# Low parts of the expert weights: two slabs per expert halved between GpSimd and VectorE, in place of one slab left whole to GpSimd

## Chip, cores and metric

The kernel runs on one core of a Trainium2 chip. The metric is the device time of one execution in microseconds (us), median over several runs. Engines are named PE (TensorE), DVE (VectorE), ACT (ScalarE), POOL (GpSimd) and SP (SyncE, which issues most of the DMAs).

## What is computed

Two transformer-like blocks run one after the other over 1024 tokens of width 1024. The change lies at the end of the second block, in its mixture of experts: 32 experts, two per token, each a gated MLP from 1024 to 512 and back. Cut to what matters:

```
def expert_block(args):
    xb, e = args
    hb = jax.nn.silu(xb @ w_g[e]) * (xb @ w_u[e])
    return hb @ w_d[e]
```

The tokens of an expert are gathered, go through `expert_block`, and come back scaled by their gates. All is float32.

## The kernel before

A float32 product is made from three matmuls of rounded operands (`mm3`, lines 133 to 135): high by high (L133), high by low (L134), low by high (L135). So each operand is split: ACT rounds it to a high part (`ehi`, by `A` on line 40), and the low part is the operand less its high part (`elo`, by `TT` on line 43).

The experts' weights come in **units**, one DMA of 1 MB each: a slab of 128 partitions by 2048 floats. An expert has six, in the order g0, g1 (gate), u0, u1 (up), d0, d1 (down). PE takes them in the order g0, g1, u0, u1 of expert e, then d0, d1 of expert e-1, then g0 of expert e+1, twelve matmuls to a unit. In the middle of g0 stand four transposes of the hidden activations `hb` of the expert before, and behind u0 and behind u1 four each of the gathered tokens `xe` of the next expert.

The order is written out by hand (`tc.manual_schedule()`): at unit i the program first splits unit i+2 (`split_unit`, `AHEAD = HB - 1 = 2`), then issues the matmuls of unit i, then the small work that hangs on it, then the load of the slab whose buffer unit i's place in the ring frees. High and low parts have three buffers each (`HB = 3`); raw slabs lie in a ring of eleven up to unit 150, of six after it. In `esplit` ACT makes `ehi`, and one engine, handed in as `eng`, makes the whole of `elo`: POOL for u1, DVE for the other five units. DVE also makes the low parts `hl` and `xl` of the activations (their first operand lies in PSUM), and the product `hb`. POOL also issues the gather of tokens (L1493) and the scatter of results (L1532), both indirect DMAs, in its own program order. SP issues the slab loads in order (`eload`, L1482); each waits until the readers of the slab that held its buffer are done.

Of the kernel before, what the change touches and what calls it, by code (L numbers as in the profile page):

```python
# [9 lines left out]
F32 = mybir.dt.float32  # L10
# [17 lines left out]
def block_kernel(  # L28
# [8 lines left out]
    pe, act, dve, pool, sp = nc.tensor, nc.scalar, nc.vector, nc.gpsimd, nc.sync  # L37

    def A(o, i, f, **kw):
        act.activation(out=o, in_=i, func=f, **kw)  # L40

    def TT(o, a, b, op, eng=None):
        (eng or dve).tensor_tensor(out=o, in0=a, in1=b, op=op)  # L43

    def TS(o, a, s1, op0, s2=None, op1=None, eng=None):
        if op1 is None:
            (eng or dve).tensor_scalar(out=o, in0=a, scalar1=s1, scalar2=None, op0=op0)
        else:
            (eng or dve).tensor_scalar(out=o, in0=a, scalar1=s1, scalar2=s2, op0=op0, op1=op1)

    def STT(o, a, s, b, op0, op1, **kw):
        dve.scalar_tensor_tensor(out=o, in0=a, scalar=s, in1=b, op0=op0, op1=op1, **kw)  # L52

    MUL, ADD, SUB, MAX, MIN, POW = (
        ALU.mult, ALU.add, ALU.subtract, ALU.max, ALU.min, ALU.pow)
# [10 lines left out]
    def bank(tag, bufs):  # L66
        return ps[0].tile([128, 512], F32, name=tag, tag=tag, bufs=bufs)

    def mmb():
        return bank("mm", 2)  # L70

    def tpb():
        return bank("tp", 2)
# [28 lines left out]
    def split(hi, lo, src, scale=None):  # L102
        if scale is None:
            A(hi, src, AF.Copy)
            TT(lo, src, hi.bitcast(F32), SUB)
        else:
            A(hi, src, AF.Identity, scale=scale)
            STT(lo, src, scale, hi.bitcast(F32), MUL, SUB)
# [22 lines left out]
    def mm3(o, l, r, start, stop):  # L131

        pe.matmul(out=o, lhsT=l[0], rhs=r[0], start=start, stop=False)  # L133
        pe.matmul(out=o, lhsT=l[0], rhs=r[1], start=False, stop=False)  # L134
        pe.matmul(out=o, lhsT=l[1], rhs=r[0], start=False, stop=stop)  # L135

    def fslice(n=HALF):

        t = big.tile([128, 2, HALF], F32R, name="fs", tag="fs", bufs=NB)
        return t[:, 0, 0:n], t[:, 1, 0:n]  # L140
# [272 lines left out]
    with ExitStack() as ad_stack:  # L413
# [3 lines left out]
        for g in range(G):  # L417
            was.append([])
            for i in range(8):
                raw = adp.tile([128, 2, 1024 // G], F32, name="wa", tag="wa", bufs=8 * G)  # L420
# [6 lines left out]
        for k in range(8):  # L427
            o = tpb()
# [6 lines left out]
        for k in range(8):  # L435
            gk = 8 // G
            j = k % gk
            if j == 0:
                acc = adp.tile([128, 2, 1024 // G], F32, name="acc", tag="acc", bufs=2)
                for i in range(8):  # L440
                    w = was[k // gk][i]
# [4 lines left out]
                o = mmb()  # L446
# [6 lines left out]
            hi, lo = fslice()  # L453
# [1008 lines left out]
    def table(pos, rhs, n, out_i):  # L1462

        o = bank("gu", 4)
        for i in range(2):
            m = ew.tile([128, 8, 128], F32R, name="mt_", tag="ys", bufs=2)
            TT(m, islot[:, None].to_broadcast([128, 8, 128]),
               pos[:, 8 * i:8 * i + 8, None].to_broadcast([128, 8, 128]), ALU.is_equal)
            for j in range(8):
                pe.matmul(out=o[:, 0:n], lhsT=m[:, j], rhs=rhs(8 * i + j), start=(i + j == 0), stop=(i + j == 8))  # L1470
        A(out_i, o[:, 0:n], AF.Identity, scale=-1.0, bias=twos)
# [8 lines left out]
    def eload(src, nm="eraw"):  # L1480
        raw = rings[nm][0].tile([128, 2048], F32, name=nm, tag=nm, bufs=rings[nm][1])
        sp.dma_start(out=raw, in_=src)  # L1482
        return raw

    def esplit(raw, eng):
        hi = ew.tile([128, 2048], F32R, name="ehi", tag="ehi", bufs=HB)
        lo = ew.tile([128, 2048], F32R, name="elo", tag="elo", bufs=HB)
        A(hi, raw, AF.Copy)
        TT(lo, raw, hi.bitcast(F32), SUB, eng=eng)
        return hi, lo  # L1490

    def gather(xe, itok):
        pool.indirect_dma_start(out=xe, out_offset=None, in_=xn_d[:, :],  # L1493
                                in_offset=bass.IndirectOffsetOnAxis(ap=itok, axis=0),
                                bounds_check=S - 1, oob_is_err=False)

    def x_tile():
        return [mo2.tile([128, 8, 128], F32R, name=n_, tag=n_, bufs=2) for n_ in ("xh", "xl")]

    def x_part(xe, xs, g):  # L1500
        tp = bank("tpe", 2)
        transpose4(tp, [xe[:, (g * 4 + i) * 128:(g * 4 + i + 1) * 128] for i in range(4)])
        split(xs[0][:, g * 4:g * 4 + 4], xs[1][:, g * 4:g * 4 + 4], tp.rearrange("p (k n) -> p k n", k=4))

    def up_half(o, xs, w, half, mid=None):

        for i in range(4):
            k = 4 * half + i
            mm3(o, (xs[0][:, k], xs[1][:, k]), [p_[:, i * 512:(i + 1) * 512] for p_ in w], k == 0, k == 7)
            if i == 1 and mid is not None:  # L1510
                mid()

    def h_tile():
        return [mo.tile([128, 4, 128], F32R, name=n_, tag=n_, bufs=2) for n_ in ("hh", "hl")]

    def h_part(tp, hb):
        transpose4(tp, [hb[:, i * 128:(i + 1) * 128] for i in range(4)])

    def y_bank():
        return ps[0].tile([128, 2, 512], F32, name="yo", tag="yo", bufs=1)  # L1520

    def down_half(yo, hs, w, half):
        for i in range(2):
            k = 2 * half + i
            for n in range(2):
                c0 = i * 1024 + n * 512
                mm3(yo[:, n], (hs[0][:, k], hs[1][:, k]), [p_[:, c0:c0 + 512] for p_ in w], k == 0, k == 3)

    def scatter(yo, irow):
        ys = ew.tile([128, D], F32, name="ys", tag="ys", bufs=2)  # L1530
        A(ys, yo.rearrange("p a n -> p (a n)"), AF.Copy)
        pool.indirect_dma_start(out=y_d[:, :], out_offset=bass.IndirectOffsetOnAxis(ap=irow, axis=0),  # L1532
                                in_=ys, in_offset=None, bounds_check=2 * S - 1, oob_is_err=False)
# [9 lines left out]
    for i in range(len(units)):  # L1543
        nm = wide[i % len(wide)] if i < WIDE else "eraw"
# [7 lines left out]
    raws = {}  # L1552
# [22 lines left out]
    parts, banks, hbs, hss, tps, xss, yos = {}, {}, {}, {}, {}, {}, {}  # L1575

    def split_unit(i):
        nm, e, half = units[i]
        parts[i] = esplit(raws.pop(i), pool if (nm, half) == ("u", 1) else dve)

    with tc.manual_schedule():
        for e in range(2):
# [5 lines left out]
        for i in range(AHEAD):  # L1588
            split_unit(i)
        for i, (nm, e, half) in enumerate(units):  # L1590
            if i + AHEAD < len(units):
                split_unit(i + AHEAD)
            w = parts.pop(i)
            if nm in "gu":
                if half == 0:
                    banks[nm, e] = bank("gu", 4)
                if (nm, half) == ("g", 0) and e:
                    def mid():
                        tps[e - 1] = bank("tpe", 2)
                        h_part(tps[e - 1], hbs.pop(e - 1))  # L1600
# [51 lines left out]
    with tc.For_i(0, rounds) as r_:  # L1652
        with tc.For_i(0, NE) as e_:
            pos = ew.tile([128, 16], F32, name="pos", tag="pos", bufs=1)
            TS(pos, posk, shift, SUB)
            ti = ew.tile([128, 2], I32, name="ti", tag="ti", bufs=1)
            table(pos, lambda j: tkr[:, j], 2, ti)
            gather(xes[0], ti[:, 0:1])
            xs = x_tile()
            for g in range(2):  # L1660
                x_part(xes[0], xs, g)
            gu = []
            for w in (w_e_gate_2, w_e_up_2):
                o = bank("gu", 4)
                for half in range(2):
                    up_half(o, xs, esplit(eload(w[bass.ds(e_, 1), half].rearrange("o p n -> (o p) n")), dve), half)
                gu.append(o)
            hb = ew.tile([128, 512], F32, name="hb", tag="hb", bufs=2)
            A(hb, gu[0], AF.Silu)
            TT(hb, hb, gu[1], MUL)  # L1670
            tp = bank("tpe", 2)
            h_part(tp, hb)
            hs = h_tile()
            split(*hs, tp.rearrange("p (k n) -> p k n", k=4))
            yo = y_bank()
            for half in range(2):
                down_half(yo, hs, esplit(eload(w_e_down_2[bass.ds(e_, 1), half].rearrange("o p n -> (o p) n")), dve),
                          half)
            scatter(yo, ti[:, 1:2])
            TS(shift, shift, 1024.0, ADD)  # L1680
        TS(shift, shift, float(C - NE * 1024), ADD)
# [51 lines left out]
```

## Time and profile before

| | us |
|---|---|
| median of 3 runs | 2148.75 |
| lowest, highest | 2148.54, 2151.77 |
| the profiled execution, its own time | 2150.52 |
| span of the profiled execution | 2148.8 |
| busy PE | 1961.3 (91% of the span) |
| busy DVE | 1446.0 (67%) |
| busy ACT | 1177.3 (55%) |
| busy POOL | 632.5 (29%) |

The experts fill the span from about 1480 to 2090 us. In all views a time is a start in us from the beginning of the span, followed by a duration; a bracket at a row's end tells how long the engine had been idle just before the instruction, and on which engine's instruction it had waited. A busy PE says little by itself, since matmuls overlap: the distance from one start to the next tells what a matmul costs.

### The profile page before, as it was taken

The numbers are of one execution on the slowest core, as the hardware profiler recorded it, in microseconds if no ns is written. First come the engines' busy times: TensorE is split into PE (matmuls) and PEld (weight loads), VectorE is DVE, ScalarE is ACT, GpSimd is POOL, SyncE is SP. The second block draws the span as 40 slices with busy tenths as digits, with TensorE's granted clock in tenths as the row PEclk, the third lists the DMA queues.
The fourth block names the chain that finished last, engine by engine and source line by source line (L and its number), as shares of the span: only waits on it lengthen the run. The fifth ranks groups of instructions, "written<-read, shape, count | busy, mean of one in ns | idle before, by whom it ended". The sixth has DMA issues, their size and how long they took to land.

```text
span 2148.8 us, 32901 instructions
## 1 busy us (share of the span) xinstructions
PE 1961.3 (91%) x12914; PEld 1653.1 (77%) x12914; DVE 1446.0 (67%) x1923; ACT 1177.3 (55%) x1868; POOL 632.5 (29%) x522
## 2 busy tenths in 40 slices
PE   3999899999999999999999999995999999999980
PEld 2878796887777988889887997894777777777760
DVE  6476774656687754686557855746777777877765
ACT  3454553445465533564335634643777777777752
POOL 3362110144453000241004300003444444344425
PEclk8999999999997999999999999996999999999995
DMA  9212334621111263212622156464999999999956
GB/s 295 70 50 57 111 90 137 193 78 40 31 40 30 60 191 90 64 45 85 191 59 59 51 161 205 157 245 178 347 366 361 379 355 357 358 360 354 360 202 240
DMA packets 218934, 381.60 MB, mean 178 GB/s; under 512 B 50165, under 2 KB 173077, under 8 KB 193177
## 3 DMA queue, kind: packets, MB, share of 16 engines
q1 hardware_dynamic: 194520, 345.79, 46.9%
q10 hardware_dynamic: 15040, 16.89, 2.3%
q0 software_dynamic: 9216, 16.80, 2.1%
q8 instruction: 102, 1.67, 0.3%
q14 instruction: 56, 0.45, 0.1%
HBM read 356.35 MB, written 39.85 MB: 184 GB/s over the span
## 4 chain that ended last, share of the span: by engine, by line
PE 51%; issue 25%; POOL 9%; DVE 7%; DMA 6%; ACT 3%; POOLq 0%; ACTq 0%; SPq 0%; DVEq 0%; another core or an unknown queue 0%
PE mm L133 11%; PE mm L134 11%; PE mm L135 11%; POOL xe L1493 3%; PE tp L189 3%; POOL y_d L1532 2%; PE z L741 1%; DMA xp<-u_d 1%; PE sc L1139 1%; PE sc L1168 1%; PE at L599 1%; PE at L601 1%; PE os L770 1%; DVE wlo L43 1%; DVE kp L43 1%
## 5 line engine op out<-in xcount | busy, mean ns | idle before, releaser
L43 DVE TENSOR_TENSOR elo<-eraw,ehi 128x2048 fp32r<-128x2048 f32 x160 | 402.0, 2528 | 131.2 <-ACT ehi L40 131.2
L40 ACT ACTIVATE ehi<-eraw 128x2048 fp32r<-128x2048 f32 x192 | 366.9, 1912 | 18.8 <-PE yo L135 12.6
L133 PE MATMUL mm<-whi,fs 128*128 128x256 f32 x1152 | 335.4, 293 | 0.9 <-ACT whi L40 0.9
L134 PE MATMUL mm<-wlo,fs 128*128 128x256 f32 x1152 | 334.4, 291 | 0.8 <-DVE wlo L43 0.8
L135 PE MATMUL mm<-whi,fs 128*128 128x256 f32 x1152 | 331.1, 289 | 0.0
L43 DVE TENSOR_TENSOR wlo<-raw,whi 128x1024 fp32r<-128x1024 f32 x156 | 198.6, 1273 | 148.3 <-ACT whi L40 146.7
L40 ACT ACTIVATE whi<-raw 128x1024 fp32r<-128x1024 f32 x156 | 164.8, 1056 | 214.8 <-PE mm L134 93.9
L133 PEld LDWEIGHTS mm<-whi,fs 128*128 128x128 f32 x1152 | 225.0, 196 | 9.0 <-issue 5.5
L134 PEld LDWEIGHTS mm<-wlo,fs 128*128 128x128 f32 x1152 | 225.6, 196 | 8.1 <-issue 6.0
L135 PEld LDWEIGHTS mm<-whi,fs 128*128 128x128 f32 x1152 | 224.2, 195 | 2.4 <-issue 2.3
L134 PE MATMUL gu<-elo,xh 128*128 128x512 f32 x512 | 207.1, 405 | 15.9 <-POOL elo L43 14.4
L133 PE MATMUL gu<-ehi,xh 128*128 128x512 f32 x512 | 208.0, 406 | 2.5 <-ACT ehi L40 2.5
L133 PE MATMUL mm<-fs,whi 128*128 128x512 f32 x480 | 197.2, 414 | 7.5 <-DVE mst L43 4.1
L135 PE MATMUL gu<-ehi,xl 128*128 128x512 f32 x512 | 202.9, 396 | 0.0
L134 PE MATMUL mm<-fs,whi 128*128 128x512 f32 x480 | 197.0, 410 | 1.2 <-DVE fs L52 1.2
L135 PE MATMUL mm<-fs,wlo 128*128 128x512 f32 x480 | 195.1, 406 | 0.0
L43 POOL TENSOR_TENSOR elo<-eraw,ehi 128x2048 fp32r<-128x2048 f32 x32 | 147.6, 4612 | 97.2 <-ACT ehi L40 97.2
L134 PEld LDWEIGHTS gu<-elo,xh 128*128 128x128 f32 x512 | 96.6, 189 | 47.1 <-POOL elo L43 24.6
L133 PEld LDWEIGHTS mm<-fs,whi 128*128 128x128 f32 x480 | 94.0, 196 | 39.4 <-issue 9.6
L133 PEld LDWEIGHTS gu<-ehi,xh 128*128 128x128 f32 x512 | 96.7, 189 | 23.8 <-ACT ehi L40 2.9
L135 PEld LDWEIGHTS gu<-ehi,xl 128*128 128x128 f32 x512 | 96.5, 189 | 21.5
L135 PEld LDWEIGHTS mm<-fs,wlo 128*128 128x128 f32 x480 | 94.2, 196 | 23.4 <-issue 4.0
(467 smaller groups left out, 4234.5 us busy)
## 6 DMA issues: line engine op xcount, KB each, us to landing
eraw<-in_w_e_up_dram SPq DMA_DIRECT2D x64, 1024.0 KB, 7.1
eraw<-in_w_e_down_dram SPq DMA_DIRECT2D x64, 1024.0 KB, 7.3
eraw<-in_w_e_gate_dram SPq DMA_DIRECT2D x64, 1024.0 KB, 7.6
raw<-in_w_in_dram SPq DMA_DIRECT2D x92, 512.0 KB, 3.8
raw<-in_w_out_dram SPq DMA_DIRECT2D x32, 512.0 KB, 3.5
wa<-in_w_ada_dram SPq DMA_DIRECT2D x16, 512.0 KB, 5.9
fy<-y_d SPq DMA_DIRECT2D x8, 1024.0 KB, 8.7
xt<-in_x_dram SPq DMA_DIRECT2D x8, 512.0 KB, 5.6
```

The costliest lines, as they stand in the source:

```text
L40: act.activation(out=o, in_=i, func=f, **kw)
L43: (eng or dve).tensor_tensor(out=o, in0=a, in1=b, op=op)
L133: pe.matmul(out=o, lhsT=l[0], rhs=r[0], start=start, stop=False)
L134: pe.matmul(out=o, lhsT=l[0], rhs=r[1], start=False, stop=False)
L135: pe.matmul(out=o, lhsT=l[1], rhs=r[0], start=False, stop=stop)
L189: pe.transpose(o[0:s.shape[-1], j * 128:j * 128 + s.shape[0]], s, ident[0:s.shape[0], 0:s.shape[0]])
L599: pe.matmul(out=ov[:, hh, ch], lhsT=full[:, hh, ch], rhs=v(ch, hh), start=True, stop=s0 is None)
L601: pe.matmul(out=ov[:, hh, ch], lhsT=qs[r, ch * 128:(ch + 1) * 128], rhs=s0[r], start=False, stop=True)
L741: pe.matmul(out=zp[:, 0:w], lhsT=qc[r, pr, t * 128:(t + 1) * 128], rhs=kc_full[r, pr, s0 * 128:s0 * 128 + w], start=True, stop=True)
L770: pe.matmul(out=os_[:, hd * 64:hd * 64 + 64], lhsT=pt[:, j * 128:(j + 1) * 128], rhs=vc_full[:, s0 + j, hd * 64:hd * 64 + 64], start=(hd = ...
L1493: pool.indirect_dma_start(out=xe, out_offset=None, in_=xn_d[:, :], in_offset=bass.IndirectOffsetOnAxis(ap=itok, axis=0), bounds_check=S - ...
L1532: pool.indirect_dma_start(out=y_d[:, :], out_offset=bass.IndirectOffsetOnAxis(ap=irow, axis=0), in_=ys, in_offset=None, bounds_check=2 * S ...
```

## The change

`esplit` takes a column `n` in place of an engine. POOL makes the low part of the columns from `n` on, DVE that of the columns before `n`. For u1 and for d1, `n` is 1024; for the other units it is 2048, so that DVE makes the whole and POOL nothing. ACT's part is the same.

```diff
-    def esplit(raw, eng):
+    def esplit(raw, n=2048):
+
         hi = ew.tile([128, 2048], F32R, name="ehi", tag="ehi", bufs=HB)
         lo = ew.tile([128, 2048], F32R, name="elo", tag="elo", bufs=HB)
         A(hi, raw, AF.Copy)
-        TT(lo, raw, hi.bitcast(F32), SUB, eng=eng)
+        if n < 2048:
+            TT(lo[:, n:], raw[:, n:], hi[:, n:].bitcast(F32), SUB, eng=pool)
+        TT(lo[:, 0:n], raw[:, 0:n], hi[:, 0:n].bitcast(F32), SUB)
         return hi, lo
...
     def split_unit(i):
         nm, e, half = units[i]
-        parts[i] = esplit(raws.pop(i), pool if (nm, half) == ("u", 1) else dve)
+        parts[i] = esplit(raws.pop(i), 1024 if (nm, half) in (("u", 1), ("d", 1)) else 2048)
```

The loop over further rounds of experts, which this input does not enter, calls `esplit` with its default and is the same as before.

POOL's queue over one expert in the middle of the stage, before (gather and scatter of the expert before, low part of u1, gather, scatter):

```order
L1493 DMA xe_14940<-xn_d,idt 128x1024 [waits DMASW6_49,PE_49]
L1532 DMA y_d<-ys,idt 2048x1024 [waits DMASW1_49,Activation_49]
L43 TENSOR_TENSOR elo<-eraw,ehi 128x2048 [waits DMAHW6_49,Activation_49]
L1493 DMA xe_14939<-xn_d,idt 128x1024 [waits DMASW0_49,PE_49]
L1532 DMA y_d<-ys,idt 2048x1024 [waits DMASW3_49,Activation_49]
```

and with the change (scatter, half of u1, half of d1, gather, scatter):

```order
L1535 DMA y_d<-ys,idt 2048x1024 [waits DMASW1_49,Activation_49]
L43 TENSOR_TENSOR elo<-eraw,ehi 128x1024 [waits DMAHW6_49,Activation_49]
L43 TENSOR_TENSOR elo<-eraw,ehi 128x1024 [waits DMAHW0_49,PE_49,Activation_49]
L1496 DMA xe_14939<-xn_d,idt 128x1024 [waits DMASW0_49,PE_49]
L1535 DMA y_d<-ys,idt 2048x1024 [waits DMASW3_49,Activation_49]
```

The 2048 columns of u1 have become 1024, and 1024 of d1 stand between them and the gather.

DVE's queue with the change, over one expert: low part of u0, `hl`, half of u1, low part of d0, `xl`, half of d1, `hb`, `xl`, low part of the next g0:

```order
L43 TENSOR_TENSOR elo<-eraw,ehi 128x2048 [waits DMAHW3_49,PE_49,Activation_49]
L43 TENSOR_TENSOR hl<-tpe,hh 128x512 [waits Activation_49]
L43 TENSOR_TENSOR elo<-eraw,ehi 128x1024 [waits DMAHW4_49,Activation_49]
L43 TENSOR_TENSOR elo<-eraw,ehi 128x2048 [waits DMAHW5_49,PE_49,Activation_49]
L43 TENSOR_TENSOR xl<-tpe,xh 128x512 [waits Activation_49]
L43 TENSOR_TENSOR elo<-eraw_15759,ehi 128x1024 [waits DMAHW6_49,Activation_49]
L43 TENSOR_TENSOR hb<-hb,gu 128x512 [waits PE_49]
L43 TENSOR_TENSOR xl<-tpe,xh 128x512 [waits Activation_49]
L43 TENSOR_TENSOR elo<-eraw_15780,ehi 128x2048 [waits DMAHW7_49,Activation_49]
```

Before, the row of u1 was not there, and that of d1 had 2048 columns; nothing else moved on DVE.

PE's queue with the change at the beginning of u1. Before, the first matmul that reads `elo` waited for POOL:

```order
L133 MATMUL gu<-ehi,xh 128x512 [waits Activation_49]
L134 MATMUL gu<-elo,xh 128x512 [waits DVE_49]
L135 MATMUL gu<-ehi,xl 128x512
L133 MATMUL gu<-ehi,xh 128x512
L134 MATMUL gu<-elo,xh 128x512
L135 MATMUL gu<-ehi,xl 128x512
L133 MATMUL gu<-ehi,xh 128x512
L134 MATMUL gu<-elo,xh 128x512 [waits Pool_49]
```

Now the first waits for DVE, whose half holds its columns, and the third, six matmuls later, for POOL. The same pair of waits stands at d1. The order of the matmuls is the same as before.

## Rows read from the trace of the kernel before

**Rows 1.** The page's first line: span of the profiled execution.

```profile
span 2148.8 us, 32901 instructions
```

**Rows 2.** Waits of PE, 1480 to 2090: total us, times, longest.

```profile
PE gu L134 <- POOL elo L43: 14.4, 32, 0.9
```

**Rows 3.** Timeline of PE: start, us, engine, line, operation, operands, idle before.

```profile
1705.22 0.39 PE L133 MATMUL gu<-ehi,xh 128*128 128x512 f32 x1
...
1714.41 0.47 PE L133 MATMUL gu<-ehi,xh 128*128 128x512 f32 x1
1715.32 0.50 PE L134 MATMUL gu<-elo,xh 128*128 128x512 f32 x1 [0.43 <-POOL elo L43]
...
1718.34 0.48 PE L133 MATMUL yo<-ehi,hh 128*128 128x512 f32 x1
1718.65 0.39 PE L134 MATMUL yo<-elo,hh 128*128 128x512 f32 x1
...
1724.03 0.39 PE L133 MATMUL gu<-ehi,xh 128*128 128x512 f32 x1
1724.26 0.40 PE L134 MATMUL gu<-elo,xh 128*128 128x512 f32 x1
...
2071.79 0.40 PE L133 MATMUL gu<-ehi,xh 128*128 128x512 f32 x1
2073.07 0.50 PE L134 MATMUL gu<-elo,xh 128*128 128x512 f32 x1 [0.89 <-POOL elo L43]
```

**Rows 4.** Timeline of POOL: first a gather before the stage, then one expert.

```profile
1478.48 0.99 POOL L1493 DMA_INDIRECT xe<-xn_d,idt  x1 [4.21 <-PE tpe L189]
...
1710.66 4.60 POOL L43 TENSOR_TENSOR elo<-eraw,ehi 128x2048 fp32r<-128x2048 f32 x1 [2.77 <-ACT ehi L40]
1718.86 2.26 POOL L1493 DMA_INDIRECT xe<-xn_d,idt  x1 [3.59 <-PE tpe L189]
```

**Rows 5.** Timeline of DVE in the same expert: `hl`, d0, d1, g0.

```profile
1710.49 0.68 DVE L43 TENSOR_TENSOR hl<-tpe,hh 128x512 fp32r<-128x512 f32 x1
1713.90 3.52 DVE L43 TENSOR_TENSOR elo<-eraw,ehi 128x2048 fp32r<-128x2048 f32 x1 [2.72 <-ACT ehi L40]
...
1717.94 2.28 DVE L43 TENSOR_TENSOR elo<-eraw,ehi 128x2048 fp32r<-128x2048 f32 x1
...
1721.34 2.27 DVE L43 TENSOR_TENSOR elo<-eraw,ehi 128x2048 fp32r<-128x2048 f32 x1
```

**Rows 6.** Timeline of ACT in the same expert: high parts of u1, d0, d1, g0.

```profile
1708.66 1.92 ACT L40 ACTIVATE ehi<-eraw 128x2048 fp32r<-128x2048 f32 x1
...
1711.95 1.91 ACT L40 ACTIVATE ehi<-eraw 128x2048 fp32r<-128x2048 f32 x1
...
1715.18 1.91 ACT L40 ACTIVATE ehi<-eraw 128x2048 fp32r<-128x2048 f32 x1
...
1719.11 1.91 ACT L40 ACTIVATE ehi<-eraw 128x2048 fp32r<-128x2048 f32 x1
```

**Rows 7.** Kernel's end: timelines of DVE and POOL; POOL by tile `x3t` (min/median/max ns).

```profile
2112.92 4.57 DVE L52 SCALAR_TENSOR_TENSOR x3t<-fy,pk,x3t 128x1024 f32<-128x1024 f32 x2
2113.40 3.01 POOL L43 TENSOR_TENSOR x3t<-x3t,nfw 128x1024 f32<-128x1024 f32 x1 [1.27 <-ACT x3t L40]
L43 POOL TENSOR_TENSOR x3t<-x3t,nfw x4: 2344/3021/3037, 2113.4 to 2140.5; 128x1024 f32<-128x1024 f32 x4
```

**Rows 8.** By tile `wlo`, earlier stages: DVE subtraction of 1024 columns (min/median/max ns).

```profile
L43 DVE TENSOR_TENSOR wlo<-raw,whi x156: 1187/1224/2287, 15.9 to 1414.7; 128x1024 fp32r<-128x1024 f32 x156
```

**Rows 9.** Windows: busy us of each engine, granted PE clock, DMA share, GB/s.

```profile
1762.00:1780.80 18.80, 18.37 (x86) 14.67 (x85) 14.79 (x10) 14.26 (x12) 8.01 (x3) 1.00 1.00 393
1686.80:1987.60 300.80, 293.82 (x1343) 234.74 (x1343) 236.72 (x145) 228.50 (x176) 128.29 (x48) 1.00 0.94 360
```

**Rows 10.** SP's waits, 1500 to 2080; landing of `eraw`, 1930 to 2060.

```profile
SPq L1482 <- DVE elo L43: 380.8, 145, 6.5
...
DMA to landing us min/median/max: 6.5/7.5/9.4
```

More of the change, by code (lines that the diff above doesn't have):

```diff
@@ L1665, in block_kernel @@
                 for half in range(2):
-                    up_half(o, xs, esplit(eload(w[bass.ds(e_, 1), half].rearrange("o p n -> (o p) n")), dve), half)
+                    up_half(o, xs, esplit(eload(w[bass.ds(e_, 1), half].rearrange("o p n -> (o p) n"))), half)
                 gu.append(o)
@@ L1676, in block_kernel @@
             for half in range(2):
-                down_half(yo, hs, esplit(eload(w_e_down_2[bass.ds(e_, 1), half].rearrange("o p n -> (o p) n")), dve),
-                          half)
+                down_half(yo, hs, esplit(eload(w_e_down_2[bass.ds(e_, 1), half].rearrange("o p n -> (o p) n"))), half)
             scatter(yo, ti[:, 1:2])
```

## Prediction

> **What bounds it now.** The page's span [rows 1] says how long, not why, so I went first to PE's waits inside the experts' stage. They are nearly one line: 32 times, once per expert, PE waits for the low part of u1 that POOL makes [rows 2]. That row counts only idle time; what a wait costs is read from starts. In the timeline of PE the first two matmuls of u1 start 0.91 us apart (1714.41 and 1715.32). The first two of d0, which also follow four transposes but wait for nothing, start 0.31 us apart [rows 3]. So an expert loses 0.91 - 0.31 = **0.60 us**. The last expert has no transposes there: 1.28 us (2071.79 to 2073.07) against the 0.23 us of a plain pair (1724.03 to 1724.26), so it loses 1.05 us [rows 3]. All else on PE is back to back: 18.81 us per expert (1705.22 to 1724.03), at a granted clock of 1.00, the 2.4 GHz level [rows 3, 9].
>
> The timeline of POOL shows why: its 2048 columns take 4.60 us and end at 1715.26, 0.06 us before PE goes on [rows 3, 4]. The timeline of DVE shows a second thing. Its low part of d0 starts at 1713.90, while POOL is still at u1, and takes 3.52 us; the next one, beside no subtraction of POOL, takes 2.28 [rows 5]. From POOL's end to its own end are 2.16 us, so during the overlap it did almost nothing. `hl`, with an operand in PSUM, starts at 1710.49, overlaps POOL as well, and keeps its 0.68 us [rows 4, 5].
>
> **Who blocks whom.** Since the change starts both engines on one slab, this decides. The end of the kernel shows both directions [rows 7]. DVE runs two operations from 2112.92 to 2117.49. POOL starts in the middle of the first, at 2113.40, and needs 3.01 us where the same operation alone takes 2.34: it had to wait 0.67 us, until 2114.07, about the end of DVE's first. DVE's second then ends 1.08 us behind POOL's end at 2116.41. So two operations that read two SBUF operands run one after the other, and the one that was waiting first goes first.
>
> The Trainium skill says the same in "SBUF — State Buffer", section "Who interferes with whom": a VectorE instruction with two SBUF inputs and a GpSimd instruction that reads SBUF exclude each other for the whole instruction, and the first to issue wins. "Perfetto Trace Analysis", section "Optimizing Scalar/DVE Operations", concludes from it that moving work between the two might not help, which speaks against this change; by it the sum below would shrink to that of the first rival.
>
> **The change, u1.** POOL's half takes 2.34 us by the one that ran alone [rows 7]; half of the 4.60 of now would be 2.30 [rows 4]. DVE's half takes 1.19 us alone [rows 8], or 1.08 behind POOL [rows 7]. The bounds for a ready first half are thus 1.19 us (POOL loses) and 2.34 + 1.08 = 3.42 us (POOL wins). At u1 DVE is at `hl` when the high part comes, so I take the upper end: POOL from 1710.66 to 1713.00, DVE done at 1714.08. PE wants it 0.31 us after its start at 1714.41, at 1714.72: **0.6 us to spare, the stall goes**. POOL's half is wanted six matmuls later still. d0 follows on DVE at about 1714.0 and, with POOL silent, ends near 1716.3 in place of 1717.4.
>
> **The change, d1.** This is the added cost. Before, DVE alone made d1 (1717.94 to 1720.22), then `hb` and `xl` in 1.12 us, and from 1721.34 g0 of the next expert, without a gap [rows 5]. Now `xl` is done by about 1716.9, ACT's high part of d1 ends at 1717.09 [rows 6], and both engines stand ready. Who goes first? Behind ACT's high part DVE's d0 started within 0.04 us (1713.86 to 1713.90), POOL's u1 within 0.08 (1710.58 to 1710.66) [rows 4 to 6]. No row shows a tie, so there are two bounds:
> - DVE first: its half ends at 1717.13 + 1.19 = 1718.32. POOL's runs to 1718.32 + 2.34 = 1720.66, beside `hb` and `xl`, which do not collide. The high part of g0, ready 0.60 us earlier than before at 1719.11 - 0.60 + 1.91 = 1720.42 [rows 6], lets DVE start g0 at 1720.66 and end it near 1722.9. PE wants it at 1724.26 - 0.60 = 1723.66: 0.7 us to spare.
> - POOL first: POOL 1717.17 to 1719.51, DVE's half done at 1720.59. Then come `hb` and `xl` (1.12 us), and g0 runs from 1721.71 to 1723.98; with the 0.06 us that PE took behind POOL it goes on at 1724.04, 0.38 us late.
>
> I take DVE first. At this place DVE has nothing left in front of it, and it wakes sooner.
>
> **What else moves.** The gather on POOL now stands behind d1's half: it would start near 1720.7 and not 1718.86 [rows 4]. Its tokens are wanted nearly two experts later, so nobody waits. It may hold DVE off g1 for about the 0.89 us that its end lay behind DVE's before (1720.22 to 1721.12) [rows 4, 5]; g1 is wanted a whole unit after g0, so I cost that at nothing; without this cover it would be up to 0.89 us per expert. SP's load behind d1 is released by POOL, some 0.4 us later than by DVE. Slabs land within 9.4 us [rows 10] and one ring turn of six units is about an expert of 18 us, so the load has several us left. PE's extra wait at the third low matmul is over before PE comes to it. SP spends 380.8 us waiting for buffers [rows 10]: loads are not what is late.
>
> **The sum.** 31 stalls of 0.60 us and one of 1.05 us are 19.6 us. In the first expert `hb` is late on DVE by itself; I leave 0.2 us there. That makes 19.4 us less than the profiled execution's own 2150.52, or 2131.1. The median of the three runs is 1.77 us lower, so the forecast is 2148.75 - 19.4 = **2129.3 us**.
>
> **Rivals.**
> - *POOL wins at d1.* PE's stall moves from u1 to the next g0 and shrinks to 0.38 us. The gain is 31 x 0.22 + 1.05 = 7.9 us: 2140.9. For it: at the kernel's end POOL, once waiting, went ahead of DVE [rows 7]. Against: the quicker start just named. This is where the skill's remark on moving work would come true.
> - *The transfers take the gain.* An expert in 18.21 us and not 18.81 asks for 360 x 18.81 / 18.21 = 372 GB/s. If the queues could give no more than the 360 of now [rows 9], nothing would be won: 2148.8. For it: the DMA share is 0.94. Against: a stretch with share 1.00 moved 393 GB/s [rows 9].
> - *The gather holds the port (slower).* Place: POOL wins d1, the gather follows at once behind DVE's half (1720.59) and keeps DVE out. From 1.34 us on (to 1721.93: g0 is due at 1721.71, and 0.22 us are left of the stall removed) the kernel is slower than before. If it kept the port for all its 2.26 us [rows 4], to 1722.85, g0 would end at 1725.12 and PE go on 0.92 us later than before: 31 x 0.92 - 1.05 = 27.5 us more, 2176.2. Against: an unhindered gather takes 0.99 us in all [rows 4], and the 2.26 holds 1.36 us of waiting for DVE.
> - *The change does nothing for u1*, if PE still waited for both halves at its first low matmul. The order has it wait for DVE's half there and for POOL's at the third, and POOL's would be in time even for the first. I give it no chance of its own.
>
> **Chances.** DVE first at d1, the forecast: 0.72. POOL first: 0.15. Transfers, or a gain given back elsewhere: 0.08. The gather, or another collision: 0.05. A measurement here tells about 0.2% (4.3 us) from no change; POOL first lies 3.6 us beyond that, and I count 0.10 of its 0.15 as faster, since its own spare times are estimates. Faster 0.82, same 0.13, slower 0.05. The range goes from 2127.5 (the stalls' full 19.6 us and a little for other runs) to 2143.0, which takes in POOL first and 2 us beside it, as the unknown order of the two at d1 wants.
>
> **What would show it.** Right: PE's waits lose the line of rows 2; u1's first two matmuls start 0.31 us apart; POOL's instructions in `elo` are 64, those at d1 near 3.5 us from start to end since they wait for DVE's 1.2; an expert takes 18.2 us. Wrong: a new line of PE waiting for DVE's `elo` at g0, with DVE's halves at d1 near 3.4 us (POOL first); ACT waiting for slabs to land (transfers); DVE's g0 or g1 near 3 us or more beside a gather (port).

## The result, and the profile after

| | before | changed |
|---|---|---|
| median, first comparison (4 and 4 runs) | 2148.64 us | 2122.81 us |
| lowest, highest | 2147.08, 2151.77 | 2118.66, 2127.94 |
| median, second comparison (17 and 6 runs) | 2148.27 us | 2126.93 us |
| profiled execution: span, granted clock | 2148.8 us, 0.949 | 2120.9 us, 0.953 |

The ratio is 0.9893, with a 95% interval from 0.9871 to 0.9916, and in the second comparison 0.9898 (0.9876 to 0.9920). The kernel became faster by about 22 us. The forecast was 2129.3 us; the first median lies 6.5 us below it and under the range, the second lies 2.4 us below it, which is also under the range (its lower end was 2127.5).

PE's waits in the experts' stage come first, as they did before (engine, what it waited for, us in total, times, longest):

```profile
PE gu L133 <- ACT ehi L40: 2.5, 1, 2.5
PE gu L134 <- DVE elo L43: 1.5, 1, 1.5
PE yo L135 <- DVE hl L43: 1.5, 1, 1.5
PE yo L133 <- ACT hh L40: 1.2, 1, 1.2
PE tpe L189 <- DVE hb L43: 0.8, 1, 0.8
```

The line of [rows 2], 32 waits for POOL, is gone, and what is left are single waits at the first and the last expert. The timeline of PE shows the same place as [rows 3]: the matmul that opens an expert, the four transposes ahead of u1, u1's first three matmuls, and the opening matmul of the next expert.

```profile
1707.51 0.39 PE L133 MATMUL gu<-ehi,xh 128*128 128x512 f32 x1
...
1716.36 0.60 PE L189 MATMUL tpe<-ident,xe 128*128 128x128 f32 x4
1716.71 0.48 PE L133 MATMUL gu<-ehi,xh 128*128 128x512 f32 x1
1717.02 0.40 PE L134 MATMUL gu<-elo,xh 128*128 128x512 f32 x1
1717.26 0.39 PE L135 MATMUL gu<-ehi,xl 128*128 128x512 f32 x1
...
1725.63 0.39 PE L133 MATMUL gu<-ehi,xh 128*128 128x512 f32 x1
```

u1's pair is now 0.31 us apart, as forecast. But an expert takes 18.12 us and not the 18.21 of the forecast: 0.69 us came off, not 0.60. (By the median over 29 experts it went from 18.83 to 18.12 us.) The third matmul tells where the difference was. Here it follows the second by 0.24 us. Before, after the stall, it stood 0.33 us behind the second of [rows 3], which started at 1715.32:

```profile
1715.65 0.40 PE L135 MATMUL gu<-ehi,xl 128*128 128x512 f32 x1
```

So PE also restarted slowly after each stall, by 0.09 us here and by 0.10 in the median of all 32, and the distance between the first two matmuls does not contain it.

The timelines of POOL (u1's half, d1's half, gather) and of DVE in the same expert answer to [rows 4] and [rows 5]:

```profile
1712.96 2.42 POOL L43 TENSOR_TENSOR elo<-eraw,ehi 128x1024 fp32r<-128x1024 f32 x1 [2.90 <-ACT ehi L40]
1719.47 3.46 POOL L43 TENSOR_TENSOR elo<-eraw,ehi 128x1024 fp32r<-128x1024 f32 x1 [4.10 <-ACT ehi L40]
1723.09 2.90 POOL L1496 DMA_INDIRECT xe<-xn_d,idt  x1 [0.16 <-PE yo L135]
```

```profile
1712.77 0.68 DVE L43 TENSOR_TENSOR hl<-tpe,hh 128x512 fp32r<-128x512 f32 x1
1713.37 3.08 DVE L43 TENSOR_TENSOR elo<-eraw,ehi 128x1024 fp32r<-128x1024 f32 x1
...
1718.58 0.68 DVE L43 TENSOR_TENSOR xl<-tpe,xh 128x512 fp32r<-128x512 f32 x1
1719.43 1.23 DVE L43 TENSOR_TENSOR elo<-eraw,ehi 128x1024 fp32r<-128x1024 f32 x1 [0.17 <-ACT ehi L40]
1720.57 0.68 DVE L43 TENSOR_TENSOR hb<-hb,gu 128x512 f32<-128x512 f32 x1
...
1722.67 4.62 DVE L43 TENSOR_TENSOR elo<-eraw,ehi 128x2048 fp32r<-128x2048 f32 x2 [0.82 <-ACT ehi L40]
```

Both orders are there in one expert. At u1 POOL starts while DVE is still at `hl`; its half takes 2.42 us, and DVE's, called at 1713.37, takes 3.08 and ends 1.07 us behind POOL. At d1 DVE starts 0.04 us ahead of POOL and takes its plain 1.23 us; POOL's half takes 3.46. All the same DVE waits 0.82 us for the next g0's high part, so there was time to spare.

The steady stretch of the stage, by windows (columns as in [rows 9]):

```profile
1500.00:2040.00 540.00, 540.00 (x2503) 437.83 (x2502) 468.04 (x300) 426.13 (x329) 286.77 (x118) 1.00 0.97 374
```

PE is busy without a gap, and the transfers give 374 GB/s where they gave 360 before.

**Where the rest came from.** The stage, from the first transposes of gathered tokens to the last low matmul of a down product, took 612.3 us before (1476.3 to 2088.6) and 591.8 after (1468.0 to 2059.8): 20.5 us less. What follows the stage took 0.9 us more (60.2 and 61.1). The remaining 8.3 us lie ahead of the stage, in instructions that the change leaves as they were. One stretch there, before and after:

```profile
650.00:700.00 50.00, 49.30 (x308) 40.30 (x309) 36.14 (x61) 25.53 (x51) 18.39 (x15) 0.73 0.14 40
```

```profile
650.00:700.00 50.00, 47.90 (x379) 40.60 (x379) 37.59 (x64) 27.09 (x53) 16.36 (x14) 0.86 0.14 42
```

The execution before had a mean granted clock of 0.73 in these 50 us and issued 308 matmuls, the changed one 0.86 and 379. Whether that belongs to the change or to the single execution is the first thing to test.

### The profile page after: what moved, and what is told of

The parts are those of the page before. It is cut to its first block, busy times and chain, and to the rows that moved or that the text cites. A ratio compares the mean times of both kernels' runs of the same rounds, so it can differ in the third digit from the quotient of the medians.

```text
span 2120.9 us, 33031 instructions
## 1 busy us (share of the span) xinstructions
PE 1942.5 (92%) x12914; PEld 1644.2 (78%) x12914; DVE 1475.0 (70%) x1955; ACT 1177.2 (56%) x1868; POOL 689.2 (32%) x554
## 4 chain that ended last, share of the span: by engine, by line
PE 76%; DVE 8%; DMA 5%; POOL 4%; issue 4%; ACT 3%; POOLq 0%; ACTq 0%; SPq 0%; DVEq 0%; another core or an unknown queue 0%
PE mm L133 11%; PE mm L134 11%; PE mm L135 11%; PE gu L134 6%; PE gu L133 5%; PE gu L135 5%; PE yo L135 3%; PE yo L133 3%; PE yo L134 3%; PE tp L189 3%; PE tpe L189 2%; DMA xp<-u_d 1%; PE sc L1139 1%; PE sc L1168 1%; PE at L599 1%
## 5 line engine op out<-in xcount | busy, mean ns | idle before, releaser
L43 DVE TENSOR_TENSOR elo<-eraw,ehi 128x2048 fp32r<-128x2048 f32 x192 | 429.6, 2263 | 81.1 <-ACT ehi L40 81.0
L43 POOL TENSOR_TENSOR elo<-eraw,ehi 128x1024 fp32r<-128x1024 f32 x64 | 188.2, 2941 | 230.4 <-ACT ehi L40 230.4
```

## Experiments

Each kernel is the changed one except for the edit shown. "First part" is the time up to the first transposes of gathered tokens, "stage" from there to the last low matmul of a down product.

### The two kernels again

No edit: the kernel before and the changed kernel, once more.

> The kernel before once more, as a control for the stages ahead of the experts, which the change does not touch. In the first pair of profiles the experts' stage (from the transposes ahead of the first expert to the last low matmul of the last) went from 612.3 to 591.8 us, and the stages ahead of it from 1476.3 to 1468.0. Theory (the 8 us ahead of the experts are the granted clock of that one execution): this run's stage takes 612 +- 1 us, and its first part falls anywhere from 1466 to 1480 us, with the shorter ones at the higher mean clock; single times spread over 5 us or more. Rival (the change itself shortens the first part, by another placement of code or data): first part 1476 +- 1 us again.

> The changed kernel once more. Theory: stage 591.8 +- 1 us, first part anywhere from 1466 to 1480 us, and with more runs the median gain comes down towards what the stage alone gives, 20 us (ratio 0.9905), from the 25.8 us of the first four. Rival (the first part is shorter by the change): first part 1468 +- 1 us, ratio 0.987 to 0.988.

The rows that bound the stage, by tile, are the transposes (min/median/max ns, first to last start) and the low matmuls, for the kernel before and for the changed one:

```profile
L189 PE MATMUL tpe<-ident,xe x256: 272/273/446, 1473.5 to 2055.1; 128*128 128x128 f32 x128
L134 PE MATMUL yo<-elo,hh x256: 389/394/397, 1509.6 to 2086.5; 128*128 128x512 f32 x128
```

```profile
L189 PE MATMUL tpe<-ident,xe x256: 272/273/448, 1476.1 to 2036.3; 128*128 128x128 f32 x128
L134 PE MATMUL yo<-elo,hh x256: 387/394/397, 1511.1 to 2066.6; 128*128 128x512 f32 x128
```

The stage takes 613.0 us before and 590.5 changed; the latter is 1.3 us under the first profile's 591.8, slightly more than the 1 us that I had allowed, and the last expert accounts for it (below). The first parts are 1473.5 and 1476.1 us: this time the changed kernel has the longer one. So the 8 us are not the change's. The median of six runs came to 2126.93 us against 2148.27, a gain of 21.3 us. The kernel before came to 2148.97 us in 12 more runs (2138.68 to 2154.63), ratio 0.9999 (0.9980 to 1.0017): no difference.

The table has the first part and the mean granted clock of the whole span for all eight profiled executions. Up to the experts they run the same instructions:

| execution | first part, us | clock | stage, us |
|---|---|---|---|
| before | 1476.3 | 0.949 | 612.3 |
| before, again | 1473.5 | 0.949 | 613.0 |
| changed | 1468.0 | 0.953 | 591.8 |
| changed, again | 1476.1 | 0.947 | 590.5 |
| u1 alone halved | 1471.8 | 0.951 | 590.4 |
| nothing on POOL | 1476.7 | 0.949 | 590.5 |
| POOL first at d1 | 1465.6 | 0.956 | 609.3 |
| u1: 1920 columns on POOL | 1473.3 | 0.953 | 604.5 |

The first part moves over 11 us and is mostly shorter where the clock was higher. The clock records of the traces show it more closely. Within the first part PE was granted the lower of its two levels, 1.2 GHz, for 154 us in the first execution of before and for 128 us in that of the changed kernel; in the shortest first part (1465.6) it was 118 us, in one of the longest (1476.1) 158. What makes the clock fall more often in one execution than in another is not shown. The stage of one kernel repeats within 1.3 us.

### u1 alone, and nothing on POOL

```diff
-        parts[i] = esplit(raws.pop(i), 1024 if (nm, half) in (("u", 1), ("d", 1)) else 2048)
+        parts[i] = esplit(raws.pop(i), 1024 if (nm, half) == ("u", 1) else 2048)
```

for the first, and for the second

```diff
-        parts[i] = esplit(raws.pop(i), 1024 if (nm, half) in (("u", 1), ("d", 1)) else 2048)
+        parts[i] = esplit(raws.pop(i), 2048)
```

> u1 is halved as in the change, d1 stays whole on VectorE. Theory (the gain is the stall at u1 alone, 0.60 us of waiting and 0.10 us of slower restart per expert; d1's half gives nothing in the steady state and costs 1.5 us at the last expert): stage 590.3 us, 1.5 us less than with the change; no wait of PE for POOL; time same as the change or up to 2 us lower. Rival (halving d1 is part of the gain, because VectorE is short of time around d1): stage longer than the change's 591.8 us, with a wait of PE for the low part of d1 or g0.

> POOL makes no low part at all; VectorE makes all six units whole. Theory (POOL's 4.6 us for u1 was the stall; VectorE needs 2.28 us for it and has 18.1 - 6 x 2.28 - 4 x 0.68 = 1.7 us per expert to spare): stage 590.3 us as with u1 alone, no wait of PE, time same as the change or up to 2 us lower. Rival (VectorE needs POOL's help, its share of 91% is too much at one place): a wait of PE for a low part on VectorE appears, stage 594 us or more.

With u1 alone: 2125.02 us, ratio 0.9897 (0.9878 to 0.9916), stage 590.4. With nothing on POOL: 2126.55 us, ratio 0.9898 (0.9875 to 0.9922), stage 590.5. Neither has a wait of PE for POOL or for DVE beyond the single ones at the ends. So d1's half earned nothing that these runs can tell, and neither did any help by POOL: what the change removed was POOL's 4.6 us on one unit. DVE with all six units (u0, `hl`, u1, d0 here):

```profile
1701.37 2.29 DVE L43 TENSOR_TENSOR elo<-eraw,ehi 128x2048 fp32r<-128x2048 f32 x1 [1.38 <-ACT ehi L40]
1703.58 0.68 DVE L43 TENSOR_TENSOR hl<-tpe,hh 128x512 fp32r<-128x512 f32 x1
1704.18 2.28 DVE L43 TENSOR_TENSOR elo<-eraw,ehi 128x2048 fp32r<-128x2048 f32 x1
1706.99 2.29 DVE L43 TENSOR_TENSOR elo<-eraw,ehi 128x2048 fp32r<-128x2048 f32 x1 [0.52 <-ACT ehi L40]
```

u1 (at 1704.18) is whole after 2.28 us where the two halves of the change needed 3.5 (1712.96 to 1716.45), and DVE still waits for ACT.

The 1.5 us that I expected these two to win at the last expert are there against the first profile of the changed kernel, but not against its second, which lost nothing there. In the last expert's turn no `xl` stands in front of d1's half, and the tie came out differently. POOL's and DVE's halves of that d1, in the first profile and then in the second:

```profile
2044.77 2.40 POOL L43 TENSOR_TENSOR elo<-eraw,ehi 128x1024 fp32r<-128x1024 f32 x1 [3.17 <-ACT ehi L40]
2044.80 3.45 DVE L43 TENSOR_TENSOR elo<-eraw,ehi 128x1024 fp32r<-128x1024 f32 x1
```

```profile
2053.09 3.50 POOL L43 TENSOR_TENSOR elo<-eraw,ehi 128x1024 fp32r<-128x1024 f32 x1 [3.19 <-ACT ehi L40]
2053.11 1.21 DVE L43 TENSOR_TENSOR elo<-eraw,ehi 128x1024 fp32r<-128x1024 f32 x1
```

In both POOL starts sooner by the profile, by 0.03 and 0.02 us, but it went first in the first one only. So starts this close do not tell who goes first. Where POOL did, `hl` of the last expert came late: it is PE's wait of 1.5 us for `hl` in the first list above, and the second profile has no such wait.

### POOL first at d1

```diff
-    def esplit(raw, n=2048):
+    def esplit(raw, n=2048, late=False):
...
+        if late:
+            dve.tensor_copy(out=late_t, in_=last_tp[-1][:, 0:512])
         TT(lo[:, 0:n], raw[:, 0:n], hi[:, 0:n].bitcast(F32), SUB)
...
-        parts[i] = esplit(raws.pop(i), 1024 if (nm, half) in (("u", 1), ("d", 1)) else 2048)
+        parts[i] = esplit(raws.pop(i), 1024 if (nm, half) in (("u", 1), ("d", 1)) else 2048,
+                          (nm, half) == ("d", 1) and e + 2 < NE)
```

> The change, with one VectorE copy of 512 columns out of PSUM (0.6 us, result not used) in front of VectorE's half of d1, so that POOL is the first to ask there; it prices the rival that POOL wins at d1. From the changed kernel's trace: POOL's half 1719.47 to 1721.89 and not 3.46 us long, VectorE's half done at 1722.97, hb and xl 1.12 us, g0 done at 1726.36, PE on at 1726.42 where it wanted 1725.86. Theory (first come, first served, for the whole instruction): a wait of PE for VectorE's g0 appears in 30 experts, 0.56 us plus 0.10 us of slower restart each, stage 591 + 20 = 611 us, so nearly all of the gain is gone. Rival (VectorE goes first whenever both wait, or the two share): POOL's half stays at 3.4 us, no wait at g0, stage 591 to 592 us.

`late` is set for d1 of all experts but the last two, and `last_tp` holds the PSUM tile of the `xl` just made. The copy (0.67 us) made POOL the first, 0.20 us ahead of DVE. PE's waits, and one expert on POOL, on DVE, and on PE at the next g0:

```profile
PE gu L134 <- DVE elo L43: 11.5, 31, 1.5
```

```profile
1705.88 2.39 POOL L43 TENSOR_TENSOR elo<-eraw,ehi 128x1024 fp32r<-128x1024 f32 x1 [3.08 <-ACT ehi L40]
```

```profile
1706.08 3.28 DVE L43 TENSOR_TENSOR elo<-eraw,ehi 128x1024 fp32r<-128x1024 f32 x1
1709.28 0.68 DVE L43 TENSOR_TENSOR hb<-hb,gu 128x512 f32<-128x512 f32 x1
```

```profile
1712.07 0.40 PE L133 MATMUL gu<-ehi,xh 128*128 128x512 f32 x1
1712.81 0.50 PE L134 MATMUL gu<-elo,xh 128*128 128x512 f32 x1 [0.34 <-DVE elo L43]
1713.14 0.39 PE L135 MATMUL gu<-ehi,xl 128*128 128x512 f32 x1
```

The durations have changed places: 2.39 us on POOL, 3.28 on DVE. The line of waits that the prediction named as its sign of being wrong is there. PE now loses 0.51 us at g0's second matmul (0.74 us in place of 0.23; expected 0.56) and 0.10 at the third. 30 x 0.61 = 18.3 us, and the stage is 609.3 us (expected 611), 17.5 to 18.8 longer than the change's. The copy itself delays nothing that I can see: DVE's half ends 1.09 us behind POOL's, much as at u1, where POOL goes first without a copy (1.07). The median is 2145.29 us against 2145.06, ratio 0.9996 (0.9973 to 1.0019). So who goes first at d1 decides over nearly the whole gain of the change, and in the changed kernel the two halves start there within 0.04 to 0.06 us of each other.

### A shorter stall

```diff
         if n < 2048:
-            TT(lo[:, n:], raw[:, n:], hi[:, n:].bitcast(F32), SUB, eng=pool)
-        TT(lo[:, 0:n], raw[:, 0:n], hi[:, 0:n].bitcast(F32), SUB)
+            TT(lo[:, 0:n], raw[:, 0:n], hi[:, 0:n].bitcast(F32), SUB, eng=pool)
+            TT(lo[:, n:], raw[:, n:], hi[:, n:].bitcast(F32), SUB)
+        else:
+            TT(lo, raw, hi.bitcast(F32), SUB)
...
-        parts[i] = esplit(raws.pop(i), 1024 if (nm, half) in (("u", 1), ("d", 1)) else 2048)
+        parts[i] = esplit(raws.pop(i), 1920 if (nm, half) == ("u", 1) else 2048)
```

> u1 as before on POOL, but only its first 1920 columns; VectorE makes the last 128, d1 whole on VectorE. POOL's piece ends 0.29 us earlier than its 4.61 us of before, so PE's stall at u1 should shrink and not vanish. Theory (a stall costs its waiting and a fixed 0.10 us of slower restart): u1's second matmul starts 0.62 us behind the first (0.31 late), the third 0.33 behind the second, 0.41 us lost per expert, stage 590.5 + 32 x 0.41 = 603.6 us. Rival (no such restart; the extra is something else in the expert): 0.31 us lost, stage 600.4 us. Rival (extra in proportion to the wait): 0.36 us, 602.0 us.

```profile
1709.18 0.47 PE L133 MATMUL gu<-ehi,xh 128*128 128x512 f32 x1
1709.82 0.50 PE L134 MATMUL gu<-elo,xh 128*128 128x512 f32 x1 [0.17 <-POOL elo L43]
1710.16 0.40 PE L135 MATMUL gu<-ehi,xl 128*128 128x512 f32 x1
1710.39 0.39 PE L133 MATMUL gu<-ehi,xh 128*128 128x512 f32 x1
```

The second matmul is 0.64 us behind the first, 0.33 late; the third 0.34 behind the second, 0.11 late. That is 0.44 us per expert, and 590.5 + 32 x 0.44 = 604.6 us; the stage measures 604.5. The restart is as slow after 0.33 us as after 0.60, so over these waits it is a fixed price. The expectation that says so (603.6, with a wait of 0.31) is 0.9 us off, the other two (600.4 and 602.0) are 4.1 and 2.5 off, more than the stage of one kernel moves. Why PE restarts slowly is not shown. The time is 2140.16 us, ratio 0.9960 (0.9941 to 0.9980).

## Why the prediction was right in kind and wrong in size

- **The stall at u1 goes**: right. The row is gone and the pair is 0.31 us apart.
- **POOL first at u1, DVE first at d1**: right, with 3.08 us for DVE's half at u1 (from POOL's start to a ready first half 3.49 us, 1712.96 to 1716.45; forecast 3.42) and 3.46 us for POOL's at d1 (forecast near 3.5). What "SBUF — State Buffer" says in "Who interferes with whom", in the Trainium skill, agrees: the second to start is held for the first one's whole instruction. Which one that is when the starts lie 0.02 or 0.03 us apart, as at the last expert, no row here tells beforehand.
- **The term that failed: "an expert loses 0.91 - 0.31 = 0.60 us".** It is 0.70: 0.60 of waiting and 0.10 of restart, which the first two matmuls don't show. With 0.70 the sum is 31 x 0.70 + 1.15 - 0.2 = 22.7 us, and the forecast would have been 2126.1 us, by itself under the range and 0.8 us from the second median. Stages of 612.3 and 613.0 us before and 590.5 after give 21.8 to 22.5. The first profile of the changed kernel (591.8) gives 20.5 to 21.2; it lost 1.5 us to the tie at the last expert, for which the sum had no term. The 0.2 us left for the first expert were measured by no run alone.
- **The bound that failed: "the stalls' full 19.6 us and a little for other runs".** Three runs of before lay within 3.2 us, and the range went only 1.8 us below the forecast. Over 17 runs the kernel before went from 2141.49 to 2154.26 us, and the first part alone moves by 11. The first four runs of the changed kernel fell low: 2122.81 us against 2126.93 of the next six. Of the 6.5 us between the forecast and the first median about 3 are the restart. The rest is no more than the first part moves: in the profiled execution, one of the four, it was 8 us shorter than before. The other three have no trace, so for them this is argued and not shown; as far as it holds, that their median lay so low was chance.
- **The gather, the transfers, SP's later release**: right that they cost nothing. The gather grew to 2.90 us and nobody waited for it; DVE's g0 beside it took 2.42 us in place of 2.28, with time to spare. The transfers moved 374 GB/s, forecast 372, without a wait of ACT for a slab.
- **The rival "POOL wins at d1"**: right in place, too cheap in price. It was put at 0.38 us per expert; with POOL made the first, 0.61 were lost, 0.51 of waiting and 0.10 of restart.
- **The remark on moving work between the two engines** ("Perfetto Trace Analysis", section "Optimizing Scalar/DVE Operations", in the Trainium skill) turned out true in a way that I had not followed up: VectorE alone does as well as any split (2126.55 us against 2126.93 of the change). I weighed it against the change and never against leaving POOL out. VectorE's time was in the rows: 2.28 us for u1 from 1711.2, behind `hl`, would have been ready at 1713.5, where PE wanted it at 1714.72.

No kernel here is faster than the change by more than the runs tell apart, and with PE's gaps in the stage gone, moving low parts between these engines has nothing left to remove there. Leaving POOL out of the splits is the simplest of the equals.

## What to carry to other kernels

When PE waits for one slow producer, look first whether the fast engine has room for the whole piece; splitting a piece over GpSimd and VectorE put the two halves one behind the other here, where both read two SBUF operands (3.5 us for both halves, 2.28 for the whole on VectorE), and the order of a tie can decide the gain. Price a stall over the matmuls behind it, not by the first pair alone. And before giving a range, ask how far the stages that a change leaves alone move from run to run: three runs can agree by chance.

## What the runs showed that was not expected

- A matmul behind a wait is followed by the next after 0.33 to 0.34 us in place of 0.23, alike after waits of 0.33, 0.51 and 0.60 us.
- With both engines waiting for the same high part, one goes first for its whole instruction: at d1 VectorE, which starts 0.04 us sooner (1.23 us against 3.46 on GpSimd), and GpSimd when it was made to start 0.20 us sooner (2.39 us against 3.28 on VectorE). At the last expert, with GpSimd 0.02 to 0.03 us sooner, either went first.
- Up to the experts the same instructions took between 1465.6 and 1476.7 us, the shorter times mostly at the higher mean granted clock: 118 us at the lower level in the shortest, 148 to 158 in the three longest.
